# Weight sums of the seven-product blocks moved between engines and transfers

## The chip, the cores and the metric

The kernel runs on one core of a Trainium2 chip. Its engines run side by side, each with a queue of its own that is worked through in order: TensorE (PE; its weight loads are listed as PEld), VectorE (DVE), ScalarE (ACT), GpSimd (POOL) and SyncE (SP), which here only issues transfers. The metric is the device time of one execution in microseconds.

## The reference, cut to what matters

A trunk of two layers on 256 tokens of 1024 channels, all in float32. Each layer is

```python
h = h + 0.5 * swiglu_ffn(rmsnorm(h, g1), w1, w3, w2)      # 1024 -> 2816 -> 1024
h = h + mixer(rmsnorm(h, gm))                             # layer 0: convolution module, layer 1: attention
h = h + 0.5 * swiglu_ffn(rmsnorm(h, g2), w1, w3, w2)
# swiglu_ffn(h, w1, w3, w2) = (silu(h @ w1) * (h @ w3)) @ w2
```

and one more rmsnorm ends it. The change touches the four feed-forward stages alone, mostly the product with `w2`.

## The kernel before, in words

**Products in three parts.** A float32 product is made of three passes of TensorE over split operands: every operand x is kept as a high part (a cast copy) and a low part (x minus the high part), and `mm3` (L269 to L275) multiplies low x high, high x high and high x low into the same sum. So every weight that arrives from DRAM costs ScalarE a copy (`hi`) and VectorE a subtraction (`lo`), in `load` (L144 to L163): each 128x2048 block is converted in two pieces of 1024 (`PIECES`).

**Two rings of buffers.** A weight block is 128 partitions x 2048 values, 1 MB. It lands in one of four `raw` buffers (`RAW_BUFS`), and its two parts lie in one of four pairs `hi`, `lo` (`W_BUFS`). A raw buffer is free again when the last conversion has read it, a pair when the last matmul has. The blocks of the whole program stand in one list (L108 onwards); `load_ahead` (L201) issues the next ones as the current one is taken by `weights` (L212). The loads are issued on SyncE's queue, in order, together with the small transfers of `turn` (below). The order of instructions on each engine is fixed when the program is built, by a scheduler's own estimate of times; `urgent` (L185) gives a function's instructions priority, and `behind` (L139) puts the conversions after the last six urgent instructions of their engine.

**A feed-forward stage.** The up half takes 22 weight blocks in six rounds (`c` = 0 to 5 in `ffn_in`): TensorE makes 128x512 results for both token halves, ScalarE and VectorE make silu(a) * b of them, and `turn` (L619) transposes each result: VectorE in 32x32 squares, then four 64 KB transfers to DRAM (`gd`) and one of 256 KB back (`gb`), after which ScalarE and VectorE split it into `Gh` and `Gl`, the left operands of the down half.

The down half (`Rows`, from L499) takes 11 weight blocks of 256 rows x 1024 columns. Its four results (two token halves x two column halves) stay in four PSUM banks. An ordinary block takes 2 x 2 x 2 products of 128x128 by 128x512, each in three passes: 24 matmuls. The blocks named in `FAST = (0, 2, 4, 6, 8)` are made with seven products in place of eight, 21 matmuls, by a Strassen-like scheme: it needs sums of the four 128x512 weight quarters and differences of the activations' quarters.

- The weight sums are in `load_fast` (L165): one 1 MB load on SyncE, a GpSimd sum of 128x1024 (two quarters at once, L172), two VectorE sums of 128x512 (L173, L174), then the conversions of `raw` and of `sums` in pieces (L180, L181). So such a block takes two raw buffers and two pairs.
- The activations' differences are in `combine` (L606): four GpSimd differences of 128x128 (L611) per block, when the second token half of round `c` is back from DRAM.
- Four of the seven products are shared by several results and are summed over all seven-product blocks in four more PSUM banks (`p`). After block 8, `fold` (L546) combines them and adds them to h: one ScalarE copy, four VectorE sums, four GpSimd sums.

Blocks 9 and 10 are done by `finish` (L561), result by result, so that the next stage's normalisation can begin under it; each result is added to h by VectorE (L566).

Of the kernel before, what the change touches and what calls it, by code (L numbers as in the profile page):

```python
# [19 lines left out]
P = 128  # L20
# [25 lines left out]
FAST = (0, 2, 4, 6, 8)  # L46
# [34 lines left out]
def trunk(ctx: ExitStack, tc: tile.TileContext, x, xt, pos, invf, gains, gfin, wdw,  # L81
# [28 lines left out]
    for i in range(2):  # L110
        for w13, w2 in ((f1w13, f1w2), (f2w13, f2w2)):
# [32 lines left out]
    def load(src, pieces=1):  # L144
        if isinstance(src, tuple) and src[0] == "fast":
            return load_fast(src[1])
        if isinstance(src, tuple):
# [17 lines left out]
    def load_fast(src):  # L165
# [3 lines left out]
        nc.sync.dma_start(raw, src)  # L169
        v = raw.rearrange("p (b n) -> p b n", n=512)  # L170
        t = sums.rearrange("p (b n) -> p b n", n=512)
        behind(nc.gpsimd.tensor_tensor(t[:, 0:2, :], v[:, 0:4:3, :], v[:, 1:2, :].to_broadcast([P, 2, 512]), op=ALU.add))  # L172
        behind(nc.vector.tensor_add(t[:, 2, :], t[:, 0, :], v[:, 3, :]))  # L173
        behind(nc.vector.tensor_add(t[:, 3, :], t[:, 2, :], v[:, 2, :]))  # L174
        out = []
        for x, cols in ((raw, ((0, 512), (1024, 2048))), (sums, ((0, 1024), (1024, 2048)))):
            hi = wp.tile([P, HB], F32R, tag="hi", name=uid("hi"))
            lo = wp.tile([P, HB], F32R, tag="lo", name=uid("lo"))
            for c0, c1 in cols:
                behind(nc.scalar.copy(hi[:, c0:c1], x[:, c0:c1]))  # L180
                behind(nc.vector.tensor_sub(lo[:, c0:c1], x[:, c0:c1], hi[:, c0:c1].bitcast(F32)))  # L181
            out.append((hi, lo))
# [316 lines left out]
    class Rows:  # L499
        def __init__(self, zh, zl, nk, last=False, sh=None, sl=None):  # L500
# [4 lines left out]
            self.early = max(i for i in range(nk // 2 - 2) if sh is None or i not in FAST)  # L505
# [21 lines left out]
        def fast(self, i):  # L527

            n = FAST.index(i)
# [6 lines left out]
            for o, key, (ah, al), (hi, lo), q in (  # L536
                    (self.p[0], "p1", z(f, 0), raw, 0), (self.o[0, 0], (0, 0), z(f + 1, 0), raw, 2),
                    (self.o[0, 1], (0, 1), s(2), raw, 3), (self.p[2], "p5", z(f, 1), sums, 0),
                    (self.p[3], "q7", s(1), sums, 1), (self.p[1], "q6", s(0), sums, 2),
                    (self.o[1, 0], (1, 0), z(f + 1, 1), sums, 3)):  # L540
                c = slice(q * 512, q * 512 + 512)
                mm3(o, ah, al, hi[:, c], lo[:, c], self.begin(key), isinstance(key, str) and i == FAST[-1])
            if i == FAST[-1]:
                self.fold()

        def fold(self):  # L546
# [5 lines left out]
            nc.gpsimd.tensor_tensor(h[0][:, left], h[0][:, left], s1, op=ALU.add)  # L552
            nc.vector.tensor_sub(v, q6, s1)
            nc.vector.tensor_add(w, p5, v)
            nc.gpsimd.tensor_tensor(h[0][:, right], h[0][:, right], w, op=ALU.add)
            nc.vector.tensor_add(y, q7, v)
            nc.gpsimd.tensor_tensor(h[1][:, left], h[1][:, left], y, op=ALU.subtract)
            nc.vector.tensor_add(z, q7, w)
            nc.gpsimd.tensor_tensor(h[1][:, right], h[1][:, right], z, op=ALU.add)
# [31 lines left out]
    def ffn(X, make_next, beside=lambda: None):  # L591
        with tc.tile_pool(name=uid("ffn"), bufs=1) as act:
            return ffn_in(act, X, make_next, beside)

    def ffn_in(act, X, make_next, beside):
        Gh = act.tile([P, NF, S], F32R, tag="Gh", name=uid("Gh"))
        Gl = act.tile([P, NF, S], F32R, tag="Gl", name=uid("Gl"))
        Sh = act.tile([P, 3 * len(FAST), P], F32R, tag="Sh", name=uid("Sh"))
        Sl = act.tile([P, 3 * len(FAST), P], F32R, tag="Sl", name=uid("Sl"))
# [6 lines left out]
        def combine(i, b0, b1):  # L606

            n = FAST.index(i)
            sx = act.tile([P, 4, P], F32, tag="sx", name=uid("sx"))
            v = sx.rearrange("p s (i q) -> p s i q", q=32)  # L610
# [5 lines left out]
            split(Sh[:, 3 * n:3 * n + 3, :], Sl[:, 3 * n:3 * n + 3, :], sx[:, :3, :])  # L616
            split(Gh[:, 2 * i, tbs(1)], Gl[:, 2 * i, tbs(1)], sx[:, 3, :])

        def turn(c, tb, w, g):  # L619
# [14 lines left out]
            t0 = 0  # L634
            if tb == 1 and 2 * c in FAST:
                t0 = 1
                combine(2 * c, first[c], bv)
            f = slice(4 * c + t0, 4 * c + n)
            gh, gl = (G_[:, f, tbs(tb)].rearrange("p t (i q) -> p t i q", q=32) for G_ in (Gh, Gl))
            split(gh, gl, bv[:, t0:])  # L640
# [49 lines left out]
        o = Rows(Gh, Gl, NF, make_next is Final, Sh, Sl)  # L690
        for i in range(NF // 2 - 2):
            (o.fast if i in FAST else o.block)(i)
# [503 lines left out]
    X = ffn(X, lambda act: Plain("mix_0", act), beside)  # L1196
# [4 lines left out]
    X = ffn(X, lambda act: Norm("ffn1_1", half=True))  # L1201
    X = ffn(X, lambda act: Norm("mix_1"))
    cc, sn = rope_tables()
    X = mla(X, lambda act: Norm("ffn2_1", half=True), cc, sn)
    ffn(X, Final)


def _layout(x, positions, ffn_norm1, ffn1_w1, ffn1_w3, ffn1_w2, mix_norm, ffn_norm2,
# [33 lines left out]
    for k in range(KT):  # L1242
# [21 lines left out]
        "f1w2": np.stack([rows(ffn1_w2[i]) for i in range(2)]),  # L1264
# [30 lines left out]
```

## Time and profile before

| | |
|---|---|
| median of 3 runs | 931.85 us (931.53 to 936.24) |
| the profiled execution | 930.08 us |
| its span, first to last instruction | 928.3 us |
| TensorE busy | 913.5 us, 98% |
| VectorE busy | 687.6 us, 74% |
| ScalarE busy | 536.4 us, 58% |
| GpSimd busy | 213.4 us, 23% |
| DMA, the queue of SyncE and its 16 engines | 190.09 MB, 58.7% busy |
| weight loads of 1 MB for the feed-forward stages, issue to landing | 4.8 and 5.3 us (median of two groups) |

The four feed-forward stages lie at about 13 to 187, 293 to 468, 468 to 648 and 744 to 925 us of the span; the convolution module stands between the first two, attention between the last two. In the profile, an instruction is named by its line and by the tiles it writes and reads: `lo<-raw,hi` at L162 is the low part of an ordinary weight block, `lo<-sums,hi` at L181 that of the sums, `p<-` a shared product, `o<-` a product of one result alone, `u<-` a product of the up half. A bracket at the end of a row is the time the engine stood idle before it, with what ended the wait. TensorE's matmuls overlap in the listing: the time of one is read from the distance of starts.

### The profile page before, as it was taken

The numbers are of one execution on the slowest core, as the hardware profiler recorded it, in microseconds if no ns is written. First come the engines' busy times: TensorE is split into PE (matmuls) and PEld (weight loads), VectorE is DVE, ScalarE is ACT, GpSimd is POOL, SyncE is SP. The second block draws the span as 40 slices with busy tenths as digits, with TensorE's granted clock in tenths as the row PEclk, the third lists the DMA queues.
The fourth block names the chain that finished last, engine by engine and source line by source line (L and its number), as shares of the span: only waits on it lengthen the run. The fifth ranks groups of instructions, "written<-read, shape, count | busy, mean of one in ns | idle before, by whom it ended". The sixth has DMA issues, their size and how long they took to land.

```text
span 928.3 us, 12409 instructions
## 1 busy us (share of the span) xinstructions
PE 913.5 (98%) x4337; PEld 761.0 (82%) x4337; DVE 687.6 (74%) x1047; ACT 536.4 (58%) x928; POOL 213.4 (23%) x325
## 2 busy tenths in 40 slices
PE   9999999899999999999999999999999999999997
PEld 7888888798977888888888888888898778888886
DVE  5777787889974667778876667878666476667975
ACT  6964465558865445455575445655667374544643
POOL 1110222349931001222210003223200010003223
PEclk9999999999999999999999999999999999999999
DMA  9986555823323866565857765657451557774651
GB/s 340 348 291 231 203 170 216 317 90 139 137 91 127 299 243 237 184 196 198 308 198 237 246 233 184 193 206 262 181 182 46 182 204 236 254 246 150 226 181 46
DMA packets 60399, 191.58 MB, mean 206 GB/s; under 512 B 11184, under 2 KB 33328, under 8 KB 40752
## 3 DMA queue, kind: packets, MB, share of 16 engines
q1 hardware_dynamic: 59760, 190.09, 58.7%
q8 instruction: 34, 0.56, 0.2%
q10 hardware_dynamic: 576, 0.69, 0.2%
q14 instruction: 29, 0.24, 0.1%
HBM read 178.17 MB, written 12.58 MB: 205 GB/s over the span
## 4 chain that ended last, share of the span: by engine, by line
PE 89%; DVE 5%; ACT 3%; DMA 1%; issue 1%; SPq 0%; POOLq 0%; ACTq 0%; POOL 0%; DVEq 0%
PE u L275 17%; PE u L271 17%; PE u L274 17%; PE o L271 6%; PE o L274 6%; PE o L275 6%; DVE lo L162 3%; PE u L717 3%; PE gate L717 3%; PE p L275 2%; PE p L271 2%; PE p L274 2%; PE o L901 2%; PE y L790 2%; ACT hi L161 1%
## 5 line engine op out<-in xcount | busy, mean ns | idle before, releaser
L162 DVE TENSOR_TENSOR lo<-raw,hi 128x1024 fp32r<-128x1024 f32 (+1 forms) x250 | 304.9, 1255 | 76.9 <-ACT hi L161 76.8
L161 ACT CAST hi<-raw 128x1024 fp32r<-128x1024 f32 (+1 forms) x250 | 248.0, 1046 | 153.3 <-PE u L275 111.1
L275 PE MATMUL u<-hi,Xl 128*128 128x512 f32 x688 | 267.8, 390 | 0.7 <-DVE Xl L330 0.7
L271 PE MATMUL u<-lo,Xh 128*128 128x512 f32 x688 | 268.1, 390 | 0.1
L274 PE MATMUL u<-hi,Xh 128*128 128x512 f32 x688 | 267.7, 389 | 0.0
L275 PEld LDWEIGHTS u<-hi,Xl 128*128 128x128 f32 x688 | 129.2, 188 | 28.5 <-DVE Xl L330 1.6
L271 PEld LDWEIGHTS u<-lo,Xh 128*128 128x128 f32 x688 | 129.2, 188 | 26.8 <-DVE lo L162 0.5
L274 PEld LDWEIGHTS u<-hi,Xh 128*128 128x128 f32 x688 | 129.2, 188 | 26.8
L271 PE MATMUL o<-lo,Gh 128*128 128x512 f32 (+1 forms) x236 | 91.0, 386 | 0.0
L275 PE MATMUL o<-hi,Gl 128*128 128x512 f32 (+1 forms) x236 | 91.0, 385 | 0.0
L274 PE MATMUL o<-hi,Gh 128*128 128x512 f32 (+1 forms) x236 | 91.0, 385 | 0.0
L172 POOL TENSOR_TENSOR sums<-raw 128x1024 f32<-128x1024 f32 x20 | 53.1, 2653 | 161.2 <-DMA raw<-in_f2w 52.6
L611 POOL TENSOR_TENSOR sx<-gb 128x128 f32<-128x128 f32 x20 | 10.4, 521 | 311.9 <-DMA gb<-gd 311.9
L181 DVE TENSOR_TENSOR lo<-sums,hi 128x1024 fp32r<-128x1024 f32 x40 | 56.1, 1433 | 0.0
L603 ACT CAST Gh<-gb 128x512 fp32r<-128x512 f32 (+2 forms) x48 | 25.6, 539 | 49.8 <-DMA gb<-gd 49.6
L761 DVE SCALAR_TENSOR_TENSOR acc<-V,dw,acc 128x256 f32<-128x256 f32 (+1 forms) x160 | 54.0, 417 | 0.1
L180 ACT CAST hi<-sums 128x1024 fp32r<-128x1024 f32 x40 | 40.7, 1052 | 22.5 <-PE u L275 15.3
L604 DVE TENSOR_TENSOR Gl<-gb,Gh 128x512 fp32r<-128x512 f32 (+2 forms) x48 | 33.1, 704 | 26.4 <-ACT Gh L603 26.4
L275 PEld LDWEIGHTS o<-hi,Gl 128*128 128x128 f32 x236 | 44.3, 188 | 9.0
L274 PEld LDWEIGHTS o<-hi,Gh 128*128 128x128 f32 x236 | 44.3, 188 | 9.0
L271 PEld LDWEIGHTS o<-lo,Gh 128*128 128x128 f32 x236 | 44.3, 188 | 8.7
L180 ACT CAST hi<-raw 128x512 fp32r<-128x512 f32 (+1 forms) x40 | 31.4, 834 | 34.7 <-PE o L275 27.8
(246 smaller groups left out, 1336.6 us busy)
## 6 DMA issues: line engine op xcount, KB each, us to landing
raw<-in_f2w SPq DMA_DIRECT2D x66, 1024.0 KB, 4.8
raw<-in_f1w SPq DMA_DIRECT2D x64, 1024.0 KB, 5.3
raw<-in_cw SPq DMA_DIRECT2D x12, 1024.0 KB, 6.0
gd<-gt SPq DMA_DIRECT2D x160, 64.0 KB, 2.5
gb<-gd SPq DMA_DIRECT2D x40, 256.0 KB, 3.0
raw<-in_wo SPq DMA_DIRECT2D x4, 1024.0 KB, 4.9
raw<-in_wuq SPq DMA_DIRECT2D x3, 1024.0 KB, 4.7
raw<-in_f1w SPq DMA_DIRECT2D x8, 256.0 KB, 6.2
```

The source lines that it names most:

```text
L161: behind(nc.scalar.copy(hi[:, c], raw[:, c]))
L162: behind(nc.vector.tensor_sub(lo[:, c], raw[:, c], hi[:, c].bitcast(F32)))
L172: behind(nc.gpsimd.tensor_tensor(t[:, 0:2, :], v[:, 0:4:3, :], v[:, 1:2, :].to_broadcast([P, 2, 512]), op=ALU.add))
L180: behind(nc.scalar.copy(hi[:, c0:c1], x[:, c0:c1]))
L181: behind(nc.vector.tensor_sub(lo[:, c0:c1], x[:, c0:c1], hi[:, c0:c1].bitcast(F32)))
L271: mm = nc.tensor.matmul(o, ah, bl, start=start, stop=False)
L274: nc.tensor.matmul(o, ah, bh, start=False, stop=False)
L275: return nc.tensor.matmul(o, al, bh, start=False, stop=stop)
L603: nc.scalar.copy(dh, x)
L604: nc.vector.tensor_sub(dl, x, dh.bitcast(F32))
L717: mm = nc.tensor.matmul(u[:, t], w[:, c], X.x[:, k, t], start=(k == 0), stop=(k == KT - 1))
L761: nc.vector.scalar_tensor_tensor(out if j == j1 - 1 else y, v, w, y, op0=ALU.mult, op1=ALU.add)
```

## The change

- **Weight sums.** `load_fast` no longer uses GpSimd's arithmetic. The host stores the quarters of these blocks in another order (`down`). SyncE loads three quarters into `raw` (768 KB) and the fourth twice, side by side, into the first half of `sums` (a broadcast read, 512 KB). Then a transfer issued by GpSimd adds two quarters from DRAM onto that half (`accum_op`, 512 KB). The other two sums stay on VectorE.
- **Conversions.** `raw` (1536 values) and `sums` (2048) are each converted in one piece, and so are the up half's blocks from round 1 on and the ordinary down blocks ("wide").
- **More seven-product blocks.** `FAST` is now a table by stage: the first stage keeps blocks 0, 2, 4, 6, 8; the other three take 0, 1, 3, 4, 6, 8.
- **Differences.** `combine` works on VectorE, one of the four in place, for either block of a round.
- **Fold.** It is urgent, its four GpSimd sums go to VectorE (the first straight from PSUM), and in the last seven-product block the four shared products come first.

```diff
-FAST = (0, 2, 4, 6, 8)
+FAST = {0: (0, 2, 4, 6, 8), 1: (0, 1, 3, 4, 6, 8), 2: (0, 1, 3, 4, 6, 8), 3: (0, 1, 3, 4, 6, 8)}
...
                 for m in range(2):
-                    blocks += [w13[i, m, 2 * cc_ + a_] for a_ in range(2)]
-            blocks += [w13[i, a_, 10] for a_ in range(2)]
-            blocks += [("fast", w2[i, a_]) if a_ in FAST else w2[i, a_] for a_ in range(NF // 2)]
+                    blocks += [("wide", w13[i, m, 2 * cc_ + a_]) if cc_ else w13[i, m, 2 * cc_ + a_]
+                               for a_ in range(2)]
+            blocks += [("wide", w13[i, a_, 10]) for a_ in range(2)]
+            blocks += [("fast" if a_ in FAST[2 * i + g_] else "wide", w2[i, a_]) for a_ in range(NF // 2)]
...
         raw = rawp.tile([P, HB], F32, tag="raw", name=uid("raw"))
         sums = rawp.tile([P, HB], F32, tag="raw", name=uid("sums"))
-        nc.sync.dma_start(raw, src)
+        nc.sync.dma_start(raw[:, :1536], src[:, :1536])
         v = raw.rearrange("p (b n) -> p b n", n=512)
         t = sums.rearrange("p (b n) -> p b n", n=512)
-        behind(nc.gpsimd.tensor_tensor(t[:, 0:2, :], v[:, 0:4:3, :], v[:, 1:2, :].to_broadcast([P, 2, 512]), op=ALU.add))
-        behind(nc.vector.tensor_add(t[:, 2, :], t[:, 0, :], v[:, 3, :]))
+        nc.sync.dma_start(t[:, 0:2, :], src[:, 1536:].unsqueeze(1).to_broadcast([P, 2, 512]))
+        nc.gpsimd.dma_start(sums[:, :1024], src[:, :1024], accum_op=ALU.add)
+        behind(nc.vector.tensor_add(t[:, 2, :], t[:, 0, :], v[:, 1, :]))
         behind(nc.vector.tensor_add(t[:, 3, :], t[:, 2, :], v[:, 2, :]))
         out = []
-        for x, cols in ((raw, ((0, 512), (1024, 2048))), (sums, ((0, 1024), (1024, 2048)))):
+        for x, n in ((raw, 1536), (sums, HB)):
             hi = wp.tile([P, HB], F32R, tag="hi", name=uid("hi"))
             lo = wp.tile([P, HB], F32R, tag="lo", name=uid("lo"))
-            for c0, c1 in cols:
-                behind(nc.scalar.copy(hi[:, c0:c1], x[:, c0:c1]))
-                behind(nc.vector.tensor_sub(lo[:, c0:c1], x[:, c0:c1], hi[:, c0:c1].bitcast(F32)))
+            behind(nc.scalar.copy(hi[:, :n], x[:, :n]))
+            behind(nc.vector.tensor_sub(lo[:, :n], x[:, :n], hi[:, :n].bitcast(F32)))
...
+            shared = [(self.p[0], "p1", z(f, 0), raw, 0), (self.p[2], "p5", z(f, 1), sums, 0),
+                      (self.p[3], "q7", s(1), sums, 1), (self.p[1], "q6", s(0), sums, 2)]
+            own = [(self.o[0, 0], (0, 0), z(f + 1, 0), raw, 2), (self.o[0, 1], (0, 1), s(2), raw, 1),
+                   (self.o[1, 0], (1, 0), z(f + 1, 1), sums, 3)]
+            end = i == self.units[-1]
+            if end:
+                order_ = [shared[0], shared[3], shared[1], shared[2], *own]
+            else:
+                order_ = [shared[0], *own[:2], *shared[1:], own[2]]
...
+        @urgent
         def fold(self):
...
             nc.scalar.copy(s1, p1)
-            nc.gpsimd.tensor_tensor(h[0][:, left], h[0][:, left], s1, op=ALU.add)
+            nc.vector.tensor_add(h[0][:, left], p1, h[0][:, left])
             nc.vector.tensor_sub(v, q6, s1)
             nc.vector.tensor_add(w, p5, v)
-            nc.gpsimd.tensor_tensor(h[0][:, right], h[0][:, right], w, op=ALU.add)
+            nc.vector.tensor_add(h[0][:, right], h[0][:, right], w)
...
-        def combine(i, b0, b1):
...
-            sub = lambda o, a, b: nc.gpsimd.tensor_tensor(o, a, b, op=ALU.subtract)
-            sub(v[:, 3], b1[:, 0], b1[:, 1])
-            sub(v[:, 0], b0[:, 0], v[:, 3])
-            sub(v[:, 1], b1[:, 0], b0[:, 0])
-            sub(v[:, 2], b0[:, 1], v[:, 0])
+        def combine(c, b0, b1):
+            for e in range(2):
+                if 2 * c + e not in units:
+                    continue
...
+                nc.vector.tensor_sub(s7, a21, a11)
+                nc.vector.tensor_sub(a21, a21, a22)
+                nc.vector.tensor_sub(s6, a11, a21)
+                nc.vector.tensor_sub(s3, a12, s6)
+                split(Sh[:, 3 * n:3 * n + 3, :], Sl[:, 3 * n:3 * n + 3, :], sx)
...
+    def down(w, units):
+        r = rows(w).reshape(NF // 2, P, 4, 512)
+        for i in units:
+            r[i] = r[i][:, [0, 3, 2, 1]]
+        return r.reshape(NF // 2, P, HB)
```

More of the change, by code (lines that the diff above doesn't have):

```diff
@@ L146, in load @@
             return load_fast(src[1])
+        if isinstance(src, tuple) and src[0] == "wide":
+            src, pieces = src[1], 1
         if isinstance(src, tuple):
@@ L504, in __init__ @@
             self.begun = set()
-            self.early = max(i for i in range(nk // 2 - 2) if sh is None or i not in FAST)
+            self.early = max(i for i in range(nk // 2 - 2) if i not in fast)
         def begin(self, key):
@@ L689, in ffn_in @@
                 turn(c, tb, w, g)
[L690 removed]
+        o = Rows(Gh, Gl, NF, make_next is Final, Sh, Sl, units)
         for i in range(NF // 2 - 2):
[L692 removed]
+            (o.fast if i in units else o.block)(i)
             beside()
```

62 lines of the change are left out of this document (28 added, 34 removed).

## The prediction

> **What bounds the kernel now.** I read the engine shares first, then the chain that ended last, then the order of time at the end of a feed-forward stage.
>
> ```profile
> PE 913.5 (98%) x4337; PEld 761.0 (82%) x4337; DVE 687.6 (74%) x1047; ACT 536.4 (58%) x928; POOL 213.4 (23%) x325
> PE 89%; DVE 5%; ACT 3%; DMA 1%; issue 1%; SPq 0%; POOLq 0%; ACTq 0%; POOL 0%; DVEq 0%
> ...
> 127.24 0.39 PE L271 MATMUL p<-lo,Gh 128*128 128x512 f32 x1
> 159.65 0.39 PE L275 MATMUL o<-hi,Sl 128*128 128x512 f32 x1
> 168.04 0.39 PE L271 MATMUL p<-lo,Gh 128*128 128x512 f32 x1
> 182.09 0.39 PE L275 MATMUL o<-hi,Gl 128*128 128x512 f32 x1
> 185.35 2.02 PE L433 MATMUL tp<-dR,h 128*128 128x128 f32 x16 [2.87 <-ACT sigm L422]
> 469.12 0.40 PE L274 MATMUL u<-hi,Xh 128*128 128x512 f32 x1
> 469.79 0.51 PE L275 MATMUL u<-hi,Xl 128*128 128x512 f32 x1 [0.28 <-DVE Xl L330]
> 470.13 0.39 PE L271 MATMUL u<-lo,Xh 128*128 128x512 f32 x1
> 648.30 0.50 PE L275 MATMUL a<-hi,Xl 128*128 128x512 f32 x1 [0.28 <-DVE Xl L330]
> ```
>
> TensorE is the bound. A matmul is listed with 0.39 us, but they overlap: from 159.65 to 182.09 there are 99 starts, so one costs 22.44/99 = 0.227 us. An ordinary down block (24 matmuls) takes 5.44 us, a seven-product block (21) 4.76 us. The rows at 127.24 and 168.04 are the starts of down blocks 0 and 8 in the first stage, 40.8 us apart: four pairs of 10.2, so nothing waits there today. The waits that a cheaper stage end could recover are three: 182.09 to 185.35 (about 3.0 us beyond one matmul), and two of about 0.6 us (469.12 to 470.13 is 1.01 us for two matmuls, 0.55 too much; likewise at 648.30). Why the first one is there:
>
> ```profile
> 142.92 2.35 DVE L181 TENSOR_TENSOR lo<-sums,hi 128x1024 fp32r<-128x1024 f32 x2
> 169.33 4.60 DVE L162 TENSOR_TENSOR lo<-raw,hi 128x1024 fp32r<-128x1024 f32 x3 [1.59 <-ACT hi L161]
> 175.58 0.68 DVE L554 TENSOR_TENSOR fold<-p,fold 128x512 f32<-128x512 f32 x1
> 176.19 0.67 DVE L556 TENSOR_TENSOR fold<-p,fold 128x512 f32<-128x512 f32 x1
> 176.78 4.18 DVE L162 TENSOR_TENSOR lo<-raw,hi 128x1024 fp32r<-128x1024 f32 x2
> 181.48 1.87 DVE L566 TENSOR_TENSOR h<-o,h 128x512 f32<-128x512 f32 x3
> 184.96 0.29 DVE L427 TENSOR_SCALAR dR<-ident,R 128x128 f32<-128x128 f32 x1 [1.61 <-POOL R L306]
> ...
> 177.60 2.28 POOL L557 TENSOR_TENSOR h<-h,fold 128x512 f32<-128x512 f32 x1
> ```
>
> The first result tile was complete about 175.5 (block 8 starts at 168.04, block 9 at 172.8, the tile needs 12 matmuls), yet its sum into h starts at 181.48, because VectorE is behind: two low parts take 4.18 us beside a GpSimd sum and 2.35 us alone (142.92).
>
> What keeps weights coming is a ring of four raw buffers, and SyncE waits for them:
>
> ```profile
> SPq L158 <- DVE lo L162: 347.5, 74, 23.9
> SPq L169 <- DVE lo L162: 65.8, 16, 5.5
> ...
> 130.98 1.18 DVE L181 TENSOR_TENSOR lo<-raw,hi 128x1024 fp32r<-128x1024 f32 x1
> 152.77 2.35 DVE L181 TENSOR_TENSOR lo<-sums,hi 128x1024 fp32r<-128x1024 f32 x2
> 155.20 6.62 SPq L158 DMA_DIRECT2D raw<-in_f1w  x2
> 147.88 1.57 ACT L180 CAST hi<-raw 128x512 fp32r<-128x512 f32 x2 [3.43 <-PE o L275]
> ```
>
> Block 6's last low part ends at 155.12 and block 9's load issues at 155.20 into that buffer. ScalarE's wait at 147.88 is for the other ring, the four hi/lo buffers, which matmuls free.
>
> **The change, part by part.** *Nine matmuls go* (six seven-product blocks instead of five in three stages): 9 x 0.227 = 2.0 us, on the path.
>
> *Stage ends.* The fold's four GpSimd sums (2 us each) become VectorE sums of 0.60 us, the fold is urgent and its four products come first in its block. VectorE then has, between block 8's shared products (its start + 2.7) and the first result tile (+7.5), eight sums (4.8 us) and at most part of a low part: the sums into h start near 175.5 instead of 181.48, and the 3.9 us chain from there to the transposes (185.35) ends before 182.09. I take all three waits: 3.0 + 2 x 0.6 = 4.2 us. Bounds: 4.2, and a loss: block 10's low part can start 2 us into block 8 (its hi/lo buffer is block 7's, and the hi copy comes first); if all eight sums stood ahead of it, it would end near + 9.8, where it is needed at + 6.1, 3.7 us a stage. Today it stands ahead (the first two of the row at 169.33), and only the fold's first sums can be ready by then, so I stay at the gain.
>
> For this part and the next, the busy time of an up half and two down halves, the load rows, and waits:
>
> ```profile
> 293.00:411.00 118.00, 118.00 (x522) 97.72 (x521) 83.81 (x97) 61.03 (x81) 15.45 (x20) 1.00 0.65 223
> 411.00:468.00 57.00, 57.00 (x255) 47.22 (x254) 48.43 (x51) 32.85 (x42) 17.52 (x13) 1.00 0.68 243
> 127.00:187.00 60.00, 57.13 (x260) 47.30 (x259) 48.60 (x51) 34.46 (x45) 18.36 (x14) 1.00 0.67 238
> 162.84 2.00 ACT L161 CAST hi<-raw 128x1024 fp32r<-128x1024 f32 x2 [0.71 <-ACT hi L180]
> raw<-in_f2w SPq DMA_DIRECT2D x66, 1024.0 KB, 4.8
> raw<-in_cw SPq DMA_DIRECT2D x12, 1024.0 KB, 6.0
> gf<-in_gfin SPq DMA_DIRECT2D x1, 512.0 KB, 3.7
> 145.23 3.42 POOL L172 TENSOR_TENSOR sums<-raw 128x1024 f32<-128x1024 f32 x1 [10.34 <-issue]
> 150.54 0.33 SPq L169 DMA_DIRECT2D raw<-in_f1w  x1
> DVE Gl L604 <- ACT Gh L603: 26.4, 18, 3.6
> DVE sums L173 <- POOL sums L172: 32.8, 16, 3.0
> ```
>
> (The windows list us, then TensorE, weight loads, VectorE, ScalarE, GpSimd busy, clock, DMA share, GB/s; the DMA rows end with KB and median us to landing.)
>
> *VectorE work.* The four differences per seven-product block come from GpSimd: at most the 0.29 us of the row at 184.96 each, 23 x 4 x 0.29 = 27 us in all. Wide low parts save a fixed part: one of 1024 alone takes 1.2, two 2.35, so I take 2.3 for 2048. The first difference now waits on VectorE for the activations' landing, and low parts are queued behind it; today VectorE waits for the same landing through ScalarE's copy, 26.4 us in 18 times, at most 3.6, under one block of 5.4, and TensorE does not notice. Cover: in the up half VectorE is busy 84 of 118 us and TensorE all of it, so 7 us a stage more stays hidden; without that cover they would cost their 27 us. A wide pair delivers its low half about 1 us later, three blocks (16 us) ahead of use: nothing. Conversions in one piece, ScalarE's copies and the 23 more SyncE issues (0.33 us each): nothing, same cover.
>
> *Two weight sums by transfer.* This is the price that decides. Today's block: load 4.8 us, GpSimd sum up to 3.4, two VectorE sums 1.3; the sums buffer is taken only when GpSimd starts. Now the sums buffer takes a 512 KB broadcast load from SyncE (0.33 + 3.7 as the gf row, with semaphores 4.2), GpSimd's queue waits for its landing and issues the accumulating transfer of 512 KB (time L, no row), then the two VectorE sums (1.3). So from the moment a raw buffer is free until the next block's sums are complete pass 5.5 + L, then 2.05 (hi) + 2.3 (lo) + 0.1 = 4.4 until TensorE can use them. With the rotation of four buffers, the sums buffer of block 4 is block 2's, that of block 6 is block 4's raw buffer, that of block 8 is block 6's, and a raw buffer is released by those very sums. So the hops chain. Times from block 0's start in the new order 7,7,4,7,7,4,7,4,7 (4 an ordinary block; starts of blocks 4, 6, 8 at 19.7, 29.9, 40.1):
> - block 2's buffer: its hi/lo buffer is freed at 2.04 (nine matmuls of block 0), hi and lo end at 6.6;
> - block 4: sums complete 12.1 + L, usable 16.5 + L, needed 21.7 (after nine matmuls);
> - block 6: usable 22.0 + 2L, needed 31.9;
> - block 8: usable 27.5 + 3L, needed 40.8 (now after three matmuls, since shared products come first).
>
> The stage's stall is the largest of L - 5.2, 2L - 9.9, 3L - 13.3: none up to L = 4.4, 1.7 at 5, 4.7 at 6, 10.7 at 8. In the first stage, which still alternates, block 2's raw low part ends at 132.16, 4.9 after block 0's start; the same hops give 3L - 15.7: none to 5.2, 2.3 at 6, 8.3 at 8.
>
> L: below, a plain 512 KB load, 3.7 + 0.33 = 4.0. Above, the old bytes fetched and the sum written as two loads in turn, 2 x 3.7 + 0.33, near 8. An accumulating transfer moves 512 KB from DRAM and takes 512 KB out of the buffer: 1024 KB, which alone is 4.8 + 0.33 = 5.1 and beside other loads, as the cw row, 6.0. Here other loads are in flight (block 4's and 5's, 2.25 MB, while block 3's sum runs), so I take 6.0. GpSimd has nothing else queued there, as its sums are gone; what waits behind the issue is only the next one.
>
> The rows have no accumulating transfer. The Trainium skill, in Collectives: The Full Stack (section on the bandwidth ceiling), says that a reduce by transfer costs not the add but two source reads; its DMA: Bandwidth & Descriptors (Anatomy of one DMA, the GpSimd path) gives 2.0 us + bytes/436 GB/s. As an estimate, 1 MB would be L = 4.4, at which nothing stalls and the kernel comes to the first rival's time; the trace's 4.8 and 6.0 for such loads are longer than that fit, so I go by the rows.
>
> **Sum.** Gains 2.0 + 4.2 = 6.2. Stalls 3 x 4.7 + 2.3 = 16.4. Net +10.2 on the profiled execution's 930.08 (span 928.3): 940.3. That execution lies 1.8 below the median of 931.85, so the median should be about 942.
>
> **Rivals.** *The transfer is hidden* (other side): L below 4.4, all four stages fed in time; 931.85 - 6.2 = 925.7. For: the ring has 3L of room up to there. Against: the 4.8 of the row for the same bytes. It decides at the point where 3L - 13.3 passes 0.5. By the skill's fit above this is the outcome; no run here shows it yet.
>
> *In between*: L from 4.6 to 5.4 costs 1.5 to 9 us of stall and ends within 0.5%.
>
> *The DMA engines become the bound.* In 411:468 they are busy 0.68 x 57 = 39 us for 243 GB/s, so at most 357 GB/s. Six blocks move 0.79 MB more each and re-read 0.52: 7.9 MB, 22 us; 61 us against 55.7 of matmuls, so 5.2 a stage; the first, with five blocks, 40 + 18 against 56, 2.3. 931.85 - 6.2 + 18 = 943.6. For: these numbers. Against: blocks 0 and 1 load in the up half, at 0.65 share. With the chain on top it would be 950 to 955.
>
> *VectorE's queue blocks.* Its order is fixed; if block 6's two sums (complete at 17.6 + 2L = 29.6) stand ahead of block 5's low part, needed at 24.5, that ends at 31.9: 7.4 a stage instead of 4.7, 950. For: VectorE waits before L173 for GpSimd today, 32.8 us in 16 times. Against: those waits cost TensorE nothing.
>
> *The stage ends stay late*: 4.2 less gained, 946.
>
> **Chances.** Hidden 0.18; in between 0.16; chain stalls as forecast 0.40 (late ends included); DMA bound 0.12; blocked queue 0.14. Half a per cent (4.7 us) is about what a measurement of this kernel can tell: faster 0.18, same 0.16, slower 0.66. The range holds hidden at its lower edge, and above reaches to L near 7.5 and the two heavy rivals together, 925 to 960; the likeliest case alone (L 5.4 to 7) is 935 to 954.
>
> **What would show it.** L is the landing time of the transfer issued by GpSimd; 6.0 or more confirms the chain. TensorE's starts of blocks 4, 6 and 8 should show gaps released by lo of sums, growing towards block 8, with VectorE waiting on the transfer before its sums, SyncE's broadcast issue waiting for the previous raw buffer, and the DMA share of the down halves near 0.9. The 3 us wait before the conv's transposes (L433 now) should be gone. TensorE must lose nine matmuls. The prediction is wrong if L is under 4.5, if loads run further ahead than the ring says, or if gaps stand elsewhere.

## The result

| | median | against before | span of the profiled execution | granted clock |
|---|---|---|---|---|
| before | 934.79 us (6 runs) | | 928.3 us | 0.998 |
| after | 1052.05 us (1047.41 to 1055.39, 6 runs) | 1.126 [1.123, 1.130] | 1053.0 us | 0.952 |

The change makes the kernel 12.6% slower. The forecast was 942, with 960 as the upper end. The direction was right, the size was off by a factor of more than ten (10 us of loss forecast, 117 measured). The executions that were profiled took 930.08 and 1054.8 us, so the accounts below, made from their spans, have 124.7 us to explain.

Where the time went, first by stage. These rows are the view of the transposes' tile, before and then after: line, operation and tiles, how often, the duration of one in ns (least, median, most), and the start of the first and of the last in us.

```profile
L433 PE MATMUL tp<-dR,h x32: 275/275/347, 185.3 to 195.4; 128*128 128x128 f32 x32
L312 PE MATMUL tp<-ident,h x64: 270/272/328, 284.8 to 747.5; 128*128 128x128 f32 x64
L312 PE MATMUL tp<-ident,cn x12: 270/272/273, 661.3 to 675.9; 128*128 128x128 f32 x12
```
```profile
L437 PE MATMUL tp<-dR,h x32: 275/306/426, 215.4 to 227.1; 128*128 128x128 f32 x32
L316 PE MATMUL tp<-ident,h x64: 270/272/332, 316.5 to 843.6; 128*128 128x128 f32 x64
L316 PE MATMUL tp<-ident,cn x12: 270/272/273, 757.3 to 772.0; 128*128 128x128 f32 x12
```

Each of these starts follows the end of a stage. The convolution's transposes begin 30.1 us later (end of the first feed-forward stage), the second stage begins 31.7 later, attention 96.0 later (so 32 each for the second and third stage), the last stage 96.1 later, and the end comes 124.7 later: 29 for the last. So every stage lost about 30 us, the first one too, whose seven-product blocks are the same five as before. The convolution lost 1.6 of it, attention next to nothing.

Now the page of after: engine shares, the queue of GpSimd's transfers, and the chain that ended last.

```profile
PE 955.5 (91%) x4328; PEld 783.7 (74%) x4328; DVE 689.5 (65%) x1011; ACT 522.9 (50%) x778; POOL 105.9 (10%) x232
q0 software_dynamic: 3312, 12.06, 6.2%
PE 45%; DMA 29%; DVE 14%; ACT 5%; issue 4%; SPq 2%; POOLq 0%; POOL 0%; ACTq 0%; DVEq 0%
```

TensorE has nine matmuls fewer (4328 instead of 4337), as foretold, and yet more busy time. The chain now runs through transfers for 29%, where it was 1%. From the starts of all 512-column matmuls of the feed-forward and projection parts, taking for each distance what is beyond 0.227 us: distances over 0.52 us, which are waits, hold 96.6 us in after and 6.0 before; those between 0.30 and 0.52 us, matmuls that run but slowly, hold 37.6 (214 of them) and 3.7 (33). That is 90.6 us of waits and 33.9 us of slow matmuls, less 2.0 for the nine: 122.5 of the 124.7. **The waits are three quarters of the loss, and the slow matmuls behind them a quarter.** This says where TensorE lost its time, not what the removal of either part would give back; for that see the experiments.

The landing times of after (issues, KB each, median us from issue to landing):

```profile
sums<-in_f2w SPq DMA_DIRECT2D x12, 512.0 KB, 3.8
sums<-in_f2w POOLq DMA_DIRECT2D x12, 512.0 KB, 7.5
sums<-in_f1w SPq DMA_DIRECT2D x11, 512.0 KB, 4.0
sums<-in_f1w POOLq DMA_DIRECT2D x11, 512.0 KB, 8.2
```

The broadcast load takes 3.8 and 4.0 us, as forecast (3.7). The accumulating transfer, L of the prediction, takes 7.5 and 8.2 at the median, where 6.0 was taken and 8 was the upper bound. In the order of time, the second stage of after; first TensorE:

```profile
442.81 0.39 PE L275 MATMUL p<-lo,Gh 128*128 128x512 f32 x1
446.16 0.50 PE L275 MATMUL o<-lo,Sh 128*128 128x512 f32 x1 [1.83 <-DVE g L698]
449.55 0.79 PE L275 MATMUL p<-lo,Gh 128*128 128x512 f32 x1 [2.43 <-DVE lo L185]
450.14 0.63 PE L278 MATMUL p<-hi,Gh 128*128 128x512 f32 x1
450.57 0.63 PE L279 MATMUL p<-hi,Gl 128*128 128x512 f32 x1
462.08 0.80 PE L275 MATMUL p<-lo,Gh 128*128 128x512 f32 x1 [5.10 <-DVE lo L185]
485.84 0.80 PE L275 MATMUL p<-lo,Gh 128*128 128x512 f32 x1 [5.61 <-DVE lo L185]
500.86 0.50 PE L275 MATMUL p<-lo,Gh 128*128 128x512 f32 x1 [3.17 <-DVE lo L185]
516.55 0.80 PE L275 MATMUL p<-lo,Sh 128*128 128x512 f32 x1 [3.55 <-DVE lo L185]
```

Two groups of waits are to be seen: one in blocks 0 and 1 (446 to 462), and one in blocks 4, 6 and 8, whose restarts are 15.0 and 15.7 us apart. A pair of blocks is 10.2 us of matmuls. And the matmuls after a wait start 0.43 us apart (450.14, 450.57), not 0.227; the clock granted from 449.55 to 452.60 is 0.50, where before had 1.00 in its down half.

What feeds blocks 3, 4, 6 and 8 is the ring of buffers: SyncE's broadcast loads, GpSimd's transfers, VectorE's sums.

```profile
452.17 0.43 SPq L176 DMA_DIRECT2D sums<-in_f2w  x1
466.86 0.38 SPq L176 DMA_DIRECT2D sums<-in_f2w  x1
481.48 0.38 SPq L176 DMA_DIRECT2D sums<-in_f2w  x1
496.50 0.38 SPq L176 DMA_DIRECT2D sums<-in_f2w  x1
...
458.11 0.88 POOL L177 DMA_DIRECT2D sums<-in_f2w  x1 [20.00 <-DVE sx L629]
471.56 0.88 POOL L177 DMA_DIRECT2D sums<-in_f2w  x1 [12.57 <-DMA sums<-in_f2w]
485.89 0.86 POOL L177 DMA_DIRECT2D sums<-in_f2w  x1 [13.46 <-DVE lo L185]
500.92 0.86 POOL L177 DMA_DIRECT2D sums<-in_f2w  x1 [14.16 <-DVE lo L185]
...
463.94 0.69 DVE L178 TENSOR_TENSOR sums<-sums,raw 128x512 f32<-128x512 f32 x1 [1.44 <-DMA sums<-in_f2w]
479.99 0.69 DVE L178 TENSOR_TENSOR sums<-sums,raw 128x512 f32<-128x512 f32 x1 [5.50 <-DMA sums<-in_f2w]
495.01 0.69 DVE L178 TENSOR_TENSOR sums<-sums,raw 128x512 f32<-128x512 f32 x1 [5.36 <-DMA sums<-in_f2w]
510.70 0.69 DVE L178 TENSOR_TENSOR sums<-sums,raw 128x512 f32<-128x512 f32 x1 [6.02 <-DMA sums<-in_f2w]
```

From GpSimd's issue to VectorE's sum pass 5.8, 8.4, 9.1 and 9.8 us. A broadcast is issued when the sums of the seven-product block before are complete (481.40 and 496.43, against issues at 481.48 and 496.50), and from one to the next pass 14.6 and 15.0 us: the prediction's hop of 5.5 + L, here 6.2 + 8.4 and 5.9 + 9.1. (The 14.7 us before them are no such hop: the buffer of the issue at 466.86 was freed by an ordinary low part.) The brackets of GpSimd's rows name various releasers, but each of the four issues came 0.7 to 0.8 us after its own broadcast had landed (at 457.34, 470.83, 485.14 and 500.25 in the trace). The 5.8 had only small transfers beside it until its last 1.5 us; during the 9.8 two loads of 1 MB were in flight. Over all 23 such transfers of after, those that met one load into `raw` landed in 6.9 us at the median (11 of them), those that met two in 9.2 (12).

The waits of blocks 0 and 1 come from elsewhere. VectorE and ScalarE of after at that time:

```profile
444.75 0.69 DVE L178 TENSOR_TENSOR sums<-sums,raw 128x512 f32<-128x512 f32 x1 [7.70 <-DMA sums<-in_f2w]
445.36 0.74 DVE L698 SCALAR_TENSOR_TENSOR g<-u,rh,s 128x512 f32<-128x512 f32 x1
446.02 0.68 DVE L179 TENSOR_TENSOR sums<-sums,raw 128x512 f32<-128x512 f32 x1
447.25 2.25 DVE L185 TENSOR_TENSOR lo<-sums,hi 128x2048 fp32r<-128x2048 f32 x1
...
456.92 0.62 ACT L614 CAST Gh<-gb 128x512 fp32r<-128x512 f32 x1 [4.67 <-DVE gb L627]
457.82 1.89 ACT L184 CAST hi<-sums 128x2048 fp32r<-128x2048 f32 x1
```

VectorE stood 7.70 us before a sum of block 1. Behind it in the queue were the last gates of the up half (445.36; TensorE waited for it until 446.16) and the low part of block 0's own sums (447.25; TensorE waited until 449.55). The late gates made the activations late, and with them the differences; ScalarE waited for those (456.92), and behind that cast stood block 1's `hi` of sums, complete since 446.70 but converted at 457.82. So the waits in blocks 0 and 1, 10.6 us together by the starts, stand in this trace behind one wait for a transfer in an in-order queue. The run with the last two sums on GpSimd (below) shows that this holds for about two thirds of them.

### The profile page after: what moved, and what is told of

Read it like the earlier page. It is cut to its first block, busy times and chain, and to the rows that moved or that the text cites. A ratio compares the mean times of both kernels' runs of the same rounds, so it can differ in the third digit from the quotient of the medians.

```text
span 1053.0 us, 12165 instructions
## 1 busy us (share of the span) xinstructions
PE 955.5 (91%) x4328; PEld 783.7 (74%) x4328; DVE 689.5 (65%) x1011; ACT 522.9 (50%) x778; POOL 105.9 (10%) x232
## 3 DMA queue, kind: packets, MB, share of 16 engines
q0 software_dynamic: 3312, 12.06, 6.2%
## 4 chain that ended last, share of the span: by engine, by line
PE 45%; DMA 29%; DVE 14%; ACT 5%; issue 4%; SPq 2%; POOLq 0%; POOL 0%; ACTq 0%; DVEq 0%
DMA sums<-in_f2w 11%; DMA sums<-in_f1w 8%; PE u L279 8%; PE u L275 8%; PE u L278 8%; DMA gd<-gt 5%; DVE lo L165 5%; DMA gb<-gd 4%; PE gate L728 3%; PE u L728 3%; DVE lo L185 2%; PE o L275 2%; PE o L278 2%; ACT hi L184 2%; PE o L279 2%
## 5 line engine op out<-in xcount | busy, mean ns | idle before, releaser
L165 DVE TENSOR_TENSOR lo<-raw,hi 128x2048 fp32r<-128x2048 f32 (+2 forms) x151 | 278.0, 1864 | 79.7 <-ACT hi L164 79.5
L164 ACT CAST hi<-raw 128x2048 fp32r<-128x2048 f32 (+2 forms) x151 | 232.8, 1572 | 152.7 <-PE u L279 111.2
L184 ACT CAST hi<-sums 128x2048 fp32r<-128x2048 f32 x23 | 43.8, 1903 | 125.8 <-DVE sums L179 111.3
L178 DVE TENSOR_TENSOR sums<-sums,raw 128x512 f32<-128x512 f32 x23 | 15.9, 692 | 124.0 <-DMA sums<-in_f2w 61.1
L279 PE MATMUL o<-hi,Gl 128*128 128x512 f32 (+1 forms) x218 | 86.1, 395 | 0.0
L614 ACT CAST Gh<-gb 128x512 fp32r<-128x512 f32 (+1 forms) x48 | 28.0, 583 | 102.9 <-DMA gb<-gd 72.1
L275 PE MATMUL p<-lo,Gh 128*128 128x512 f32 x46 | 23.2, 505 | 60.9 <-DVE lo L185 60.9
L185 DVE TENSOR_TENSOR lo<-sums,hi 128x2048 fp32r<-128x2048 f32 x23 | 52.5, 2284 | 28.8 <-ACT hi L184 28.7
L275 PEld LDWEIGHTS p<-lo,Gh 128*128 128x128 f32 x46 | 9.8, 212 | 69.0 <-DVE lo L185 67.7
L790 ACT ACTIVATE prod<-V,dw 128x128 f32<-128x128 f32 (+1 forms) x121 | 45.7, 420 | 3.0 <-POOL Y L791 1.6
```

The costliest lines, as they stand in the source:

```text
L164: behind(nc.scalar.copy(hi[:, c], raw[:, c]))
L165: behind(nc.vector.tensor_sub(lo[:, c], raw[:, c], hi[:, c].bitcast(F32)))
L178: behind(nc.vector.tensor_add(t[:, 2, :], t[:, 0, :], v[:, 1, :]))
L184: behind(nc.scalar.copy(hi[:, :n], x[:, :n]))
L185: behind(nc.vector.tensor_sub(lo[:, :n], x[:, :n], hi[:, :n].bitcast(F32)))
L275: mm = nc.tensor.matmul(o, ah, bl, start=start, stop=False)
```

## The experiments

**The transfer alone, in the kernel before.** Only the two weight sums by transfer are taken over, with the order of the quarters that they need; five alternating blocks, differences, fold and conversions in pieces stay as before.

```diff
-        nc.sync.dma_start(raw, src)
+        nc.sync.dma_start(raw[:, :1536], src[:, :1536])
...
-        behind(nc.gpsimd.tensor_tensor(t[:, 0:2, :], v[:, 0:4:3, :], v[:, 1:2, :].to_broadcast([P, 2, 512]), op=ALU.add))
+        nc.sync.dma_start(t[:, 0:2, :], src[:, 1536:].unsqueeze(1).to_broadcast([P, 2, 512]))
+        nc.gpsimd.dma_start(sums[:, :1024], src[:, :1024], accum_op=ALU.add)
...
```

> The kernel before with nothing changed but the two weight sums by transfer (and the order of the quarters in DRAM). Chain theory: the loss is all here, as in the first stage of the changed kernel with about 25 us a stage: 1020 to 1060. If the loss needs the rest of the change beside it (differences and fold on VectorE, wide low parts), below 985.

Measured: 1039.28 us, 1.114 [1.110, 1.118] against 932.91. The transfer alone costs 106 us of the 117; all other parts together add some 11 to 13 us.

**All parts but the transfer.** The sums on VectorE, or on GpSimd as before, with the changed kernel's blocks, differences, fold and conversions.

```diff
-        nc.sync.dma_start(raw[:, :1536], src[:, :1536])
+        nc.sync.dma_start(raw, src)
...
-        nc.sync.dma_start(t[:, 0:2, :], src[:, 1536:].unsqueeze(1).to_broadcast([P, 2, 512]))
-        nc.gpsimd.dma_start(sums[:, :1024], src[:, :1024], accum_op=ALU.add)
+        behind(nc.vector.tensor_add(t[:, 0:2, :], v[:, 0:2, :], v[:, 3:4, :].to_broadcast([P, 2, 512])))
```

(For the second run `nc.vector.tensor_add` of the last line is a sum on GpSimd.)

> The changed kernel with one 1 MB load per seven-product block and all four weight sums on VectorE: the two transfers are undone, all else of the change stays (six blocks in three stages, wide low parts, differences and fold on VectorE). If the transfers are the whole loss, the prediction's gains of 6.2 us are left: 924 to 928 against 932. If VectorE is too full where two seven-product blocks follow each other (6.3 us of sums and low parts a block against 4.76 of matmuls), waits of 1 to 3 us a stage: 930 to 940.

> As the one before, but the first two weight sums on GpSimd, as in the kernel before the change. VectorE is slowed beside GpSimd (4.18 us for two low parts against 2.35), but has 1.2 us less to do a block: within 3 us of the VectorE form if VectorE has room, 3 to 10 us better if it has not, worse if GpSimd's 2.4 to 3.4 us lie on the path.

Measured: on VectorE 936.06, 1.004 [1.002, 1.006]; on GpSimd 957.41, 1.026 [1.024, 1.029]. With VectorE's sums the other parts are worth nothing, slightly less: the 6.2 us of gains never came. Putting the first sum back on GpSimd costs 21 us more, while the kernel before has the same sum on GpSimd and loses nothing by it. In its trace TensorE's waits of over 0.7 us for weights all stand in the three later stages, which have neighbouring seven-product blocks (in the second 2.5 us in block 1 and 3.6 in block 4), and none in the first, which has not. So the neighbouring blocks 0, 1 and 3, 4 are the likely reason, but no run shows that by itself.

**Alternating blocks with the transfer.** `FAST` is (0, 2, 4, 6, 8) in all stages.

```diff
-FAST = {0: (0, 2, 4, 6, 8), 1: (0, 1, 3, 4, 6, 8), 2: (0, 1, 3, 4, 6, 8), 3: (0, 1, 3, 4, 6, 8)}
+FAST = {i: (0, 2, 4, 6, 8) for i in range(4)}
```

> The changed kernel with blocks 0, 2, 4, 6, 8 in every stage, so that no two seven-product blocks are neighbours. Chain theory: one hop of about 15 us for each pair of blocks remains in all four stages, so little is won: 1035 to 1060. If the neighbouring blocks are what the ring cannot feed, the three later stages come near 57 to 62 us a down half: 980 to 1010.

Measured: 1038.5, 1.113 [1.109, 1.118]. The six blocks are not the cause; they account for the 11 to 13 us above (1052.05 against 1038.5), and the transfer with alternating blocks costs the same with the other parts as without them.

**A plain transfer in place of the accumulating one.**

```diff
-        nc.gpsimd.dma_start(sums[:, :1024], src[:, :1024], accum_op=ALU.add)
+        nc.gpsimd.dma_start(sums[:, :1024], src[:, :1024])
```

> The changed kernel with the transfer issued by GpSimd a plain 512 KB copy instead of an accumulating one, so the weight sums are left out (two quarters stand where their sums should). If accumulating is the price (double engine time per byte: 12.06 MB took 6.2% of the span against 196 MB in 54.5%), the landing falls from 7.5 to 8.2 us to about 4.5 to 5.5 and the time to 975 to 1000; if the price is the path through GpSimd and the wait for the broadcast load before it, landing stays at 7 or more and the time above 1030.

Measured: 1000.26, 1.073 [1.066, 1.081] against 932.17. Its queue and its landing times:

```profile
q0 software_dynamic: 3312, 12.06, 3.5%
...
sums<-in_f2w POOLq DMA_DIRECT2D x12, 512.0 KB, 5.4
sums<-in_f1w POOLq DMA_DIRECT2D x11, 512.0 KB, 5.8
```

For the same 12.06 MB the accumulating transfers hold the DMA engines 6.2% of a longer span, 65 us against 35: 1.9 times. The Trainium skill says in Collectives: The Full Stack (the section on the bandwidth ceiling), of the adds of a collective, that it is not the add that costs but the two source reads it needs; the trace agrees, with 1.9 times the engine time. Landing 2.1 to 2.4 us sooner takes 52 us off, 5 to 6 us a stage for each us of L. Landing and time lie at the upper edge of the first theory. But even a plain copy of the same size at the same place costs 68 us, so the place in the chain is dearer than the addition.

**The order of the queues.** `sums` is taken first, and its broadcast load and accumulating transfer are issued ahead of the load of `raw`; once with the changed kernel's blocks, once also with alternating ones.

```diff
-        raw = rawp.tile([P, HB], F32, tag="raw", name=uid("raw"))
         sums = rawp.tile([P, HB], F32, tag="raw", name=uid("sums"))
-        nc.sync.dma_start(raw[:, :1536], src[:, :1536])
+        raw = rawp.tile([P, HB], F32, tag="raw", name=uid("raw"))
...
         nc.gpsimd.dma_start(sums[:, :1024], src[:, :1024], accum_op=ALU.add)
+        nc.sync.dma_start(raw[:, :1536], src[:, :1536])
```

> The changed kernel with the two raw buffers of a seven-product block taken in the other order, sums first, and the broadcast load issued before the three quarters: the sums buffer is then an ordinary block's old one and is free long before the previous seven-product block's sums are complete. Chain theory (broadcast load, accumulating transfer and two sums in series from block to block, 15 us a hop): the hop falls to that of the three-quarter load, 5.8 + 1.4 us, and the waits of the later blocks go; 960 to 990. Theory of the engines as the bound: the same bytes, so within 15 us of 1052. Theory of VectorE's queue alone: the first two waits of a stage stay, the later ones too; 1030 to 1055.

> The changed kernel with the sums buffer taken first and blocks 0, 2, 4, 6, 8 in every stage: the shortest chain that the two transfers can have here. Each block then needs broadcast load, accumulating transfer and sums (4 + 6 + 1.4 us) once in 10.2 us of matmuls without waiting for the block before. If that chain from block to block was the loss, 940 to 960; if the transfers disturb in another way too (VectorE standing before them, loads slowed beside them), 965 to 985 as with six blocks.

Measured: 984.89, 1.057 [1.053, 1.061], and with five blocks 959.99, 1.028 [1.024, 1.032]. The landing times and GpSimd's queue of the first, then its engine shares in a window from its second down half to just behind its end (window in us, its length, then TensorE, weight loads, VectorE, ScalarE, GpSimd busy, clock, DMA share, GB/s):

```profile
sums<-in_f2w POOLq DMA_DIRECT2D x12, 512.0 KB, 5.9
sums<-in_f1w POOLq DMA_DIRECT2D x11, 512.0 KB, 6.2
...
464.64 0.86 POOL L176 DMA_DIRECT2D sums<-in_f2w  x1 [11.61 <-DVE sums L179]
...
442.00:500.00 58.00, 51.46 (x223) 40.93 (x222) 41.06 (x44) 28.19 (x38) 4.08 (x10) 0.97 0.76 254
```

The same bytes and the same additions, in another order and into the other buffer of each block, cost 67 us less, as the chain theory expected: L falls to about 6 at the median, and the waits by the starts from 96.6 to 44.8 us. With alternating blocks 27.9 are left. No run separates the shorter L from the earlier buffer. The DMA engines are now busy 0.76 where after has them at 0.67, so they had not been the bound. The bracket at 464.64 names a VectorE sum, but the broadcast of the same block landed at 463.88, and in this run too every issue of GpSimd comes 0.6 to 0.8 us after its own broadcast. So load and accumulation still follow one another, and some stay long beside other loads (the broadcast issued at 443.67 took 7.8 us, the accumulation issued at 439.37 took 10.8); that is a part of what remains.

**The last two sums on GpSimd**, so that VectorE doesn't stand before the transfer.

```diff
-        behind(nc.vector.tensor_add(t[:, 2, :], t[:, 0, :], v[:, 1, :]))
-        behind(nc.vector.tensor_add(t[:, 3, :], t[:, 2, :], v[:, 2, :]))
+        behind(nc.gpsimd.tensor_tensor(t[:, 2, :], t[:, 0, :], v[:, 1, :], op=ALU.add))
+        behind(nc.gpsimd.tensor_tensor(t[:, 3, :], t[:, 2, :], v[:, 2, :], op=ALU.add))
```

> The changed kernel with the two remaining weight sums on GpSimd instead of VectorE, so that VectorE no longer stands in front of the accumulating transfer with low parts queued behind. Queue theory: the waits at the start of each down half (5 to 6 us twice a stage) go, about 40 us less, near 1010; chain theory: the hop gets about 1 us longer for the slower sums, the later waits stay or grow, 1035 to 1065.

Measured: 1039.67, 1.116 [1.109, 1.122]. Some 10 to 12 us come back. GpSimd's queue now waits instead (the larger of two groups of waits: total us, times, longest), and behind these waits stand its next transfers, so this does not price VectorE's queue alone. The second row is the only longer wait of TensorE in blocks 0 and 1 of the second stage.

```profile
POOL sums L178 <- DMA sums<-in_f2w: 86.6, 12, 8.7
...
452.24 0.80 PE L275 MATMUL p<-lo,Gh 128*128 128x512 f32 x1 [4.18 <-DVE lo L185]
```

The gates are on time here, and the waits of blocks 0 and 1 fall from 30.7 to 10.6 us in the three later stages together: so about two thirds of them go when VectorE no longer stands before the transfer. The rest is not explained by its queue: ScalarE's cast of block 1's sums still stands behind activations that land late. And the waits of blocks 4, 6 and 8 grow from 36.3 to 48.9 us, so most of what is won early is waited later, as the chain theory said.

**TensorE kept busy in the waits**: twelve more matmuls of 512 columns, with zeros, ahead of the first product that needs the sums.

```diff
...
-            for o, key, (ah, al), (hi, lo), q in order_:
+            for at, (o, key, (ah, al), (hi, lo), q) in enumerate(order_):
+                if at == (1 if end else 3):
+                    for _ in range(12):
+                        nc.tensor.matmul(self.p[1 if end else 0], still[:, :P], still, start=False, stop=False)
```

> The changed kernel with twelve extra matmuls of zeros into an open sum (512 columns, at 0.227 us each 2.7 us, at half clock 5.1) in each of the 23 seven-product blocks, at the place where TensorE waits for the sums; results unchanged. Clock theory (the 34 us that TensorE loses in matmuls at 0.427 us after a wait are lost for the end): waits shrink by what the zeros take, the clock stays up, time falls by 20 to 34 us to about 1020 to 1030. Chain theory (the arrival of the sums paces the stage, slow matmuls only fill the time until the next arrival): the waits move but the stage does not get shorter by more than the part of the clock loss that lies behind the last wait; 1035 to 1060.

Measured: 1059.38, 1.137 [1.133, 1.141]. The clock view of this kernel (after has 0.952):

```profile
core 0: 1058.2 us, clock 0.977
```

The added matmuls are 23 x 12 x 0.227 = 63 us; the time grows by 7. The clock rises; counted as above, slow matmuls fall from 37.6 to 28.7 us (22.5 of it among the kernel's own matmuls, the rest among the zeros), and the waits from 96.6 to 58.3. So the zeros mostly took the place of waiting, and the chain kept its length. As slow matmuls remained, the run doesn't price them by themselves; it shows that keeping TensorE busy in this way wins nothing back here, although the clock came back in part.

**What the other parts are worth.** First, the kernel without the transfer and with alternating blocks; then the same with the order of the last two blocks changed in the first stage alone; then that last edit alone in the kernel before.

```diff
-            parts = weights(2)
+            parts = weights(2, not self.first)
```

(`first` is set for the stage whose results go to the convolution. There `finish` no longer draws the loads and conversions of the convolution's first weights ahead of its sums into h.)

> All weight sums on VectorE from one load (as in the first such run), and blocks 0, 2, 4, 6, 8 in every stage. If neighbouring seven-product blocks are what VectorE cannot feed (the waits of 1.3 to 1.6 us before the sums of the second and fourth seven-product block in the three later stages), those 6 us go, at the price of 2.0 us for nine matmuls: 930 to 933, 3 to 5 less than with six. If the waits have another cause, 936 to 940.

> As the one before, and at the end of the first stage the convolution's first two weight blocks are issued after the last sums into h, so that their four low parts (4.6 us) no longer stand ahead of these sums on VectorE. If that queue is why the first stage's end still waits 3.3 us, 2.5 to 3.3 us less than without: 927 to 930. If the wait has another cause, no difference; if the later loads are missed, up to 5 us more.

> The kernel before the change with only that move of two weight blocks at the end of the first stage. Queue theory: the fold's GpSimd sums stay, so part of the wait stays; 0.5 to 3 us less than before. If the fold on GpSimd alone holds the sums into h, no difference.

Measured: 932.48, 0.9985 [0.997, 1.000]; 931.45, 0.998 [0.996, 1.000]; and 930.21, 0.996 [0.994, 0.997] against 934.68 for before: **the last is the fastest kernel of this study**, though by less than the half per cent that a measurement was reckoned to tell; its interval lies below 1. The stage's end on TensorE: without the transfer and alternating, with the edit as well, and with the edit alone.

```profile
185.45 0.82 PE L436 MATMUL tp<-dR,h 128*128 128x128 f32 x5 [3.17 <-DVE dR L430]
```
```profile
183.73 2.05 PE L436 MATMUL tp<-dR,h 128*128 128x128 f32 x16 [0.41 <-DVE dR L430]
```
```profile
181.53 0.40 PE L275 MATMUL o<-hi,Gl 128*128 128x512 f32 x1
181.77 1.95 PE L433 MATMUL tp<-dR,h 128*128 128x128 f32 x16
...
L312 PE MATMUL tp<-ident,h x64: 270/272/329, 284.0 to 747.4; 128*128 128x128 f32 x64
```

The changed fold leaves the wait of 3.17 us in place; the order of VectorE's queue takes it to 0.41, and with the old fold on GpSimd it is gone. But in the profiled executions little of it arrives: with the edit alone the second stage's transposes begin at 284.0 instead of 284.8, and the span is 928.2 instead of 928.3. The convolution gives the 3 us back. So the wait was VectorE's queue, as expected, but the time was not: of the 2.5 to 3.3 us forecast beside the changed fold the medians show 1.0, and the edit alone shows 4.5 where at most 3 were forecast. Where these 4.5 us come from is not shown by the profiles and stays open.

## Why the prediction was wrong

The step that failed is the term "Stalls 3 x 4.7 + 2.3 = 16.4". The chain of buffers behind it is there, but it was sized with an L of 6.0, where the second stage has 8.4 to 9.8 from block 4 on; the waits of blocks 0 and 1 and the slow matmuls after each wait were put at nothing; and the first stage was held to be nearly safe. In its place TensorE lost 90.6 us in waits and 33.9 us in slow matmuls, about 30 us in each of the four stages. Term by term:

- **Nine matmuls, 2.0 us**: they went, but the time did not come. Without the transfer, six blocks measured 936.06 (1.004 of before) and five 932.48 (0.9985): neighbouring blocks cost waits of 1.3 to 1.6 us in four places, more than they save. One of them, in the kernel with the sums on VectorE:

```profile
613.98 0.50 PE L274 MATMUL p<-lo,Gh 128*128 128x512 f32 x1 [1.09 <-DVE lo L184]
```

- **Stage ends, 4.2 us**: wrong. The step that failed here is "VectorE then has ... eight sums and at most part of a low part". In the first stage of after these rows stand ahead of the sums into h:

```profile
207.14 4.62 DVE L165 TENSOR_TENSOR lo<-raw,hi 128x1024 fp32r<-128x1024 f32 x4
211.68 1.88 DVE L577 TENSOR_TENSOR h<-o,h 128x512 f32<-128x512 f32 x3
```

  Four low parts, behind all eight sums of the fold. They are those of the convolution's first two weight blocks, drawn ahead (in this kernel only they are still converted in pieces of 1024 there), while the sum reckoned with block 10's alone. The rows at 169.33 and 176.78 of before held them already: only the first two of these five low parts are block 10's. The wait stayed (3.5 us by the starts), and so did both of 0.6.
- **Differences and conversions at nothing**: held within half a per cent (the kernels of 936.06 and 932.48 have them all, with the new fold).
- **The hop of 5.5 + L and the chain of buffers**: the mechanism was right, L was not. The 6.0 rested on a plain load beside others; measured are 8.4 to 9.8 from block 4 of the second stage on. With L = 9 the prediction's own 3L - 13.3 is 13.7 us a stage, and the waits of blocks 4, 6 and 8 in the second stage are 13.6 by the starts. In the third stage they are 13.3, in the fourth 9.5. The agreement is better than the reasoning deserves, and partly luck: the hop was 5.9 to 6.2 + L and not 5.5, the waits of blocks 0 and 1 shift both sides, and the three waits do not grow towards block 8 as foretold (6.1, 3.3 and 4.1 in the second stage). Why L was long can be seen in the landing times: it is no constant of 512 KB, but goes with the loads in flight beside it (6.9 us with one, 9.2 with two), and it fell when the order was exchanged.
- **Blocks 0 and 1, not in the sum at all**: 10.6 us in the second stage. This is the rival "VectorE's queue blocks", which had the right mechanism in the wrong place: not a low part of block 5 but the gates and activations stand behind the sum. It was set against the chain as an alternative; both happened. With the sums off VectorE about a third of these waits stayed, and what causes that third is open.
- **The clock, not thought of**: after each longer wait matmuls run at half speed (granted clock 0.50), in the second stage 8.8 us. Waits of 24.6 and 8.8 of slow matmuls, less 0.7 for the three matmuls saved and 0.7 that the stage had before, are the 32 us that it lost.
- **The first stage, +2.3**: it lost 30. Its alternation did not protect it; with the same order in all stages the four lost 106 us together.
- **DMA engines as the bound**: rejected; the down half of after shows a share of 0.67, below the 0.9 it would take:

```profile
442.00:532.00 90.00, 68.31 (x255) 53.66 (x254) 57.16 (x56) 32.33 (x29) 3.48 (x4) 0.87 0.67 204
```

- **The range**: it let L vary but kept everything else in step. Its upper end should have come from L at its bound of 8 in all stages (3 x 10.7 + 8.3 = 40), with the queue's 7.4 a stage on top (22): 932 - 6 + 62 = 988. Even that is 64 us short of what was measured.

## What to carry to other kernels

A sum moved from an engine into a transfer is priced by how long it holds its buffer and by who stands behind it, not by the engine time it frees: count issue to landing at its worst among the loads around it, then follow that hop through the ring of buffers. A wait for a transfer in an in-order queue belongs behind everything that other engines need sooner. The order in which a block takes its buffers and issues its transfers is worth a try before the transfers themselves are given up: here it was worth 67 us. And where one engine's queue is late at a stage's end, look which instructions stand ahead of the needed one before moving work off other engines.

## What was not expected of the hardware

- **The price of an accumulating transfer depends on its company.** 512 KB onto SBUF landed in 5.8 us beside small transfers and in 9.8 beside two loads of 1 MB; over all of after in 6.9 at the median beside one load and 9.2 beside two; with the order exchanged, 5.9 to 6.2. A plain one at the same place took 5.4 to 5.8, a broadcast of the same size by SyncE 3.8 to 4.0.
- **Short waits cost twice.** After waits of some 2 us and more (in after all but one, at 192.89), 6 to 14 matmuls of 512 columns started 0.43 us apart instead of 0.227, most often the very next ones, otherwise after two to six fast ones. The Trainium skill, in TensorE: Matmul & The Clock Gate (Part 1), gives 426.7 ns for the halved clock, and the trace agrees; it puts the halving after an idle window of about 3.4 us, and here the rows at 449.55 to 450.57 show it after an idle time of 2.43 us (with another of 1.83 us shortly before).
- **Filling the waits kept TensorE fast only in part, and won no time**: with twelve matmuls of zeros in the waits the granted clock rose from 0.952 to 0.977 and 28.7 us of slow matmuls were left of 37.6, while the time grew by 7 us.
